# A decoder block in fp32 on one core: five running sums per pair of down-projection blocks, copies on ScalarE, the residual stored over three blocks

## Chip, cores and metric

One core of one Trainium2 chip runs the whole program in one launch. The metric is the device time of one execution in microseconds, the median of several runs. The core has TensorE (matrix products, "PE", with its weight loads "PEld"), VectorE ("DVE"), ScalarE ("ACT"), GpSimd ("POOL") and SyncE ("SP"), each with a queue that is worked off in order. Data moves between chip memory (HBM) and the on-chip SBUF by 16 DMA engines. Matrix products land in PSUM, eight banks of 128 x 512 fp32.

## The reference

A decoder block over 512 tokens of width 2048: RMS norm, one input projection, two kinds of attention, an output projection, then a gated feed-forward layer and a last RMS norm. Only the end matters here:

```python
h = h + mixed @ w_out[l]
hn2 = rmsnorm(h, norm2_g[l])
h = h + (jax.nn.silu(hn2 @ w_gate[l]) * (hn2 @ w_up[l])) @ w_down[l]
return rmsnorm(h, final_g)
```

`w_gate` and `w_up` are 2048 x 5632, `w_down` is 5632 x 2048, all fp32. Tokens stand in the free dimension, so an activation tile is 128 features x 512 tokens; token halves are called LO and HI (256 each).

## The kernel before

**Numbers.** Every fp32 operand is split into a high and a low part (`h` by a ScalarE copy that rounds, line 142 or 165; `l` by a VectorE subtraction, line 145 or 169). A product is three matmuls: high x high, low x high, high x low (`mm`, lines 1210 to 1212). A matmul is 128 x 128 weights by 256 or 512 columns.

**Gate and up blocks.** The 5632 hidden features are 44 blocks f = 0 to 43. The gate and up products of a block are computed by a scheme with seven products P1 to P7 instead of eight, with sums of weight quarters and of activation quarters. A block reads four raw weight units of 128 x 1024 (A11, A21, A22, A12). VectorE forms the sums of weight quarters in place (`comb`, line 811); `fetch` (line 815) is another way to do it: a GpSimd DMA that adds a piece from HBM onto a tile in SBUF. A product is two "halves" of 12 matmuls each. Products P2 and P3 go on in the banks of P1 and P6, and ScalarE seeds the banks of P6 and P7 with copies (line 1362). `after(f, name)` takes the banks out: for P2, VectorE multiplies bank P1 by the row of reciprocal norms `r2` into `g` (line 1282), one half later. The order of the seven products is `ORDER0` for f = 0, `ORDER1` (P2 third) for f = 1 and 2, `ORDER` (P2 sixth) afterwards.

**Splits ahead.** `next_half` splits the weights of three halves ahead before the matmuls of a half are issued, and starts loads of raw units on SP (`load_to`, five buffers). `later(n, f)` runs `f` n halves later, `soon(n, f)` n products of the down stage later. This is the only order there is: each engine's queue holds its instructions as these calls made them.

**Down stages.** Hidden features are collected over four blocks. For each group of four, the product with `w_down` follows: for the first group sixteen plain blocks in f = 4 (`down`), for nine later groups a stage at f = 8, 12, ..., 40 of eight pairs of output blocks k = 0 to 7, again with seven products each (`down7`), six matmuls per product, the products of neighbouring k interleaved. Four banks serve a k: after P1 ScalarE copies bank b1 into b2, after P6 b2 into b3 (the seeds). Results go to a staging tile of 128 x 1024 (`stg`, three buffers): ScalarE copies three of four quarters (line 1150), VectorE adds two times to make the others (line 1147), and a GpSimd DMA adds the tile onto `kept_sums[k]` in HBM (line 1166, 512 KB). `hidden_terms` makes the activation sums for a stage in a tile of the same three buffers.

**The residual.** `put_away(nb)` scales one of 16 residual blocks `hs` on VectorE and stores it in `kept_sums` by SP (lines 1316 to 1322). Eight are done one per half after product P5 of f = 1, eight after P5 of f = 2; the last one closes the pool of `hs` and opens the pool with the staging tiles. `bring_back(nb)` loads them again in f = 41 and 42, and `last` adds the products of the last group and normalises.

```python
        elif name == "P7":
            soon(1, add(s[3], b3, s[1]))
        elif name == "P3":
            soon(1, add(s[1], b2, s[1]))
        elif name == "P4":
            soon(1, copy(s[2], b3))
            soon(2, lambda: pool_e.dma_start(kept_sums[k], sums[k], accum_op=OP.add))
```

Of the kernel before, what the change touches and what calls it, by code (L numbers as in the profile page):

```python
# [11 lines left out]
F32 = mybir.dt.float32  # L12
# [4 lines left out]
S = 512  # L17
# [57 lines left out]
def block_kernel(ctx: ExitStack, tc: tile.TileContext, xt, wst, wdn, smalls, wg, w2c, bias, ident_in, out):  # L75
# [6 lines left out]
    wp = ctx.enter_context(tc.tile_pool(name="wp", bufs=1))  # L82
    ps = ctx.enter_context(tc.tile_pool(name="ps", bufs=1, space=bass.MemoryType.PSUM))
    mem = ctx.enter_context(tc.tile_pool(name="mem", bufs=1, space=bass.MemoryType.DRAM))
    kept_sums = [mem.tile([128, 2 * S], F32, name=f"sums{k}") for k in range(8)]

    def placed(pool, n, at, **kw):

# [714 lines left out]
    def quad_jobs(f, order):  # L803

        u = units.index(("quad", f, 0))

        def q(i, k):
            return raws[u + i][:, 512 * k:512 * k + 512]

        def comb(o, x):  # L810
            return lambda: dve.tensor_tensor(o(), o(), x(), op=OP.add)  # L811

        def fetch(o, i, k):

            return lambda: pool_e.dma_start(o(), wst[u + i][:, 512 * k:512 * k + 512], accum_op=OP.add)

        def nxt(i):
            return lambda: load_to(u + 4 + i + 1)

        r = {}  # L820
        for k in range(2):
            A11, A21, A22, A12 = (lambda i=i, k=k: q(i, k) for i in range(4))

            if f == 0:
                r["P1", k] = Job(A11, load=None if k else nxt(-1), post=fetch(A11, 1, k))
                r["P5", k] = Job(A21, post=fetch(A21, 0, k))
                r["P7", k] = Job(A11)
                r["P2", k] = Job(A12)
                r["P4", k] = Job(A22, prep=comb(A12, A21))
                r["P6", k] = Job(A21)  # L830
                r["P3", k] = Job(A12)
            else:
                r["P1", k] = Job(A11, post=comb(A11, A21))
                r["P4", k] = Job(A22, post=comb(A21, A22))
                r["P6", k] = Job(A22, prep=comb(A22, A11))
                r["P5", k] = Job(A21)
                r["P7", k] = Job(A11)
                r["P2", k] = Job(A12)
                r["P3", k] = Job(A12, prep=comb(A12, A22))
        if f + 1 < FB:  # L840
            if f == 0:
                r["P6", 1].post = nxt(2)
                r["P3", 1].post = nxt(3)
            else:
                r["P7", 1].post = nxt(RB - 3)
                r["P3", 1].post = nxt(RB - 1)
        else:
            r["P7", 1].post = lambda: load_fin(RB - 2)
            r["P3", 1].post = lambda: load_fin(RB)
        r["P1", 0].even = f == 2 or f % 2 == 1  # L850
        return [r[p, k] for p in order for k in range(2)]
# [4 lines left out]
    ORDER1 = ("P1", "P4", "P2", "P6", "P5", "P7", "P3")  # L856

    def order(f):
        return ORDER0 if not f else ORDER1 if f < 3 else ORDER

    def dn_job(p, nb):
        return Job(lambda: dn[p, nb], post=load_dn)
# [235 lines left out]
    banks["P5"] = ps.tile([128, 512], F32, tag="o", name="P5")  # L1098
    dbanks = {}
    SEEDED = ("P6", "P7")  # L1100

    def product(f, name):
        key = {"P2": "P1", "P3": "P6" if f else "P3"}.get(name, name)
# [25 lines left out]
    def down7(p, k, name, wh, wl):  # L1129

        if not roles:
            seed = ps.tile([128, 512], F32, tag="misc", name="pd")
            pe.matmul(seed[:, :256], ones, sm[:, :1].to_broadcast([128, 256]), start=True, stop=True)
            roles.append((banks["P3"], banks["P4"], seed, dbanks[1]))
            roles.append((banks["P1"], banks["P5"], banks["P7"], banks["P6"]))
        b1, b2, b3, b4 = (b[:, :256] for b in roles[k % 2])
        o = {"P1": b1, "P2": b1, "P6": b2, "P3": b2, "P7": b3, "P4": b3, "P5": b4}[name]
        th, tl = parts[name]
        for i in range(2):
            c = slice(128 * i, 128 * i + 128)  # L1140
            mm(o, wh[:, c], wl[:, c], th[:, i, :], tl[:, i, :], i == 0 and name in ("P1", "P5"), i == 1)
        if name == "P2":
            sums[k] = st["pool"].tile([128, 1024], F32, tag="stg", name="stg", bufs=3)
        s = [sums[k][:, 256 * q:256 * q + 256] if k in sums else None for q in range(4)]

        def add(o, a, b):
            return lambda: dve.tensor_tensor(o, a, b, op=OP.add)

        def copy(o, a):
            return lambda: act.activation(o, a, AF.Copy)  # L1150

        if name == "P1":
            copy(b2, b1)()
        elif name == "P6":
            copy(b3, b2)()
        elif name == "P2":
            soon(1, copy(s[0], b1))
        elif name == "P5":
            soon(1, copy(s[1], b4))
        elif name == "P7":  # L1160
            soon(1, add(s[3], b3, s[1]))
        elif name == "P3":
            soon(1, add(s[1], b2, s[1]))
        elif name == "P4":
            soon(1, copy(s[2], b3))
            soon(2, lambda: pool_e.dma_start(kept_sums[k], sums[k], accum_op=OP.add))  # L1166

    def hidden_terms(i, top, bot):

        x3 = st["x3"]  # L1170
        hl = [[a[:, 12:16, :].rearrange("p t (i c) -> p t i c", c=256)[:, :, i, :] for a in (ah, al)],
              [a.rearrange("p (t i c) -> p t i c", i=2, c=256)[:, :, i, :] for a in x3]]
        t = st["pool"].tile([128, 1024], F32, tag="stg", name="tt", bufs=3)
        t = [t[:, 256 * q:256 * q + 256] for q in range(4)] + [t]

        def two(q):
            return t[4][:, 512 * q:512 * q + 512].rearrange("p (t c) -> p t c", c=256)

        botv = bot.rearrange("p (t c) -> p t c", c=256)

        def hi(w, a, b, src):
            act.activation(hl[w][0][:, a:b, :], src, AF.Copy)

        def lo(w, a, b, src):
            dve.tensor_tensor(hl[w][1][:, a:b, :], src, hl[w][0][:, a:b, :].bitcast(F32), op=OP.subtract)

        def s1():
            dve.tensor_tensor(t[0], top[:, LO], top[:, HI], op=OP.subtract)
            dve.tensor_tensor(t[1], bot[:, HI], top[:, HI], op=OP.subtract)
            hi(0, 0, 2, botv)  # L1190
            hi(1, 2, 3, top[:, None, LO])

        def s2():
            dve.scalar_tensor_tensor(t[2], t[1], -1.0, top[:, LO], op0=OP.mult, op1=OP.subtract)
            dve.scalar_tensor_tensor(t[3], t[2], -1.0, bot[:, LO], op0=OP.mult, op1=OP.subtract)
            hi(0, 2, 4, two(0))
            lo(0, 0, 2, botv)
            lo(1, 2, 3, top[:, None, LO])

        def s3():  # L1200
            hi(1, 0, 2, two(1))
            lo(0, 2, 4, two(0))

        def s4():
            lo(1, 0, 2, two(1))

        return [s1, s2, s3, s4]
# [40 lines left out]
    def after(f, name):  # L1248
# [30 lines left out]
            sub(u[:, LO], x("P7"), u[:, LO])  # L1279
            add(u[:, HI], x("P7"), g[:, HI])  # L1280
        elif name == "P2":
            dve.tensor_tensor(g[:, LO], x("P1"), st["r2"][:, LO], op=OP.mult)  # L1282
            if f == FB - 1:
                finish(f, g, u, LO)
        elif name == "P3":
# [7 lines left out]
    def down(ph, nb):  # L1293
# [9 lines left out]
                   al[:, 12 + i, c], i == 0, i == PH - 1)  # L1303

        def add():
            t = st["pool"].tile([128, 1024], F32, tag="stg", name="stg", bufs=3)[:, :512]
            act.activation(t, p, AF.Copy, scale=1.0 if nb < 8 else -1.0)
            pool_e.dma_start(mem_at(nb), t, accum_op=OP.add)

        later(1, add)  # L1310

    def mem_at(nb):
        c = 512 * (nb // 8)
        return kept_sums[nb % 8][:, c:c + 512]

    def put_away(nb):
        h = hs[:, nb, :]
# [1 line left out]
            dve.tensor_tensor(h, h, st["inv"], op=OP.mult)  # L1319
        else:  # L1320
            dve.scalar_tensor_tensor(h, h, -1.0, st["inv"], op0=OP.mult, op1=OP.mult)
        sp.dma_start(mem_at(nb), h)
        if nb == KB - 1:
            rest["hsp"].close()
            st["dnp"] = ExitStack()
            pool = st["pool"] = st["dnp"].enter_context(tc.tile_pool(name="dnp", bufs=1))
            st["x3"] = [placed(pool, 3 * S, at, name="x3" + x) for x, at in (("h", MH), ("l", ML))]
            for name, x, n in (("P2", 0, 0), ("P3", 0, 1), ("P5", 0, 2), ("P7", 0, 3), ("P6", 1, 0), ("P4", 1, 1), ("P1", 1, 2)):
                parts[name] = tuple((b[:, S * n:S * n + S] if x else a[:, 12 + n, :]).rearrange("p (i c) -> p i c", c=256)
# [2 lines left out]
    def bring_back(nb):  # L1332
        if nb == 0:
            st["dnp"].close()
            st["hs"] = ctx.enter_context(tc.tile_pool(name="fin", bufs=1)).tile([128, KB, S], F32, name="hs")
        sp.dma_start(st["hs"][:, nb, :], mem_at(nb))

    for kind, a, b in sched:
        if kind == "d":
# [10 lines left out]
            continue  # L1350
        f, name = a, b
        product(f, name)
        if name == "P5" and f in (1, 2):
            for n in range(8):
                later(n, lambda nb=8 * (f - 1) + n: put_away(nb))
        if name == "P5" and f in (FB - 3, FB - 2):
            for n in range(8):
                later(n, lambda nb=8 * (f - FB + 3) + n: bring_back(nb))
        if f and name in ("P1", "P6"):
            o = {"P1": "P6", "P6": "P7"}[name]  # L1360
            st[o] = banks[o]
            act.activation(st[o][:, :256], st[name][:, :256], AF.Copy)
# [172 lines left out]
```

## Time and profile before

| | |
|---|---|
| time, median of 3 runs | 2181.99 us (2180.06 to 2184.23) |
| the profiled execution | 2184.53 us, span 2182.8 us |
| granted TensorE clock | 0.998 |
| PE / DVE / ACT / POOL busy | 99% / 78% / 54% / 5% |
| moved by DMA | 282.65 MB |

A share of busy time is over the span. Ends of matmuls are modelled, so they overlap in the rows (281 ns each, one every 113 ns). In a group of instructions stand: line, engine, operation, output and inputs by the program's names, shapes, count, then busy us, mean ns of one, the engine's idle time just before them and what ended it. In a row of waits stand: who waited, for whom, us in total, times, longest us. In a timeline row: start, duration, and in brackets the idle time before it and who ended it.

### The profile page before, as it was taken

Reading aid. Unit: us, or ns where it says so; the run is one execution under the profiler, and the core shown is the slowest. Engines: PE = TensorE matmul, PEld = TensorE weight load, DVE = VectorE, ACT = ScalarE, POOL = GpSimd, SP = SyncE. Lnnn points to the kernel's source line nnn. Section 1 sums busy time; section 2 is a strip of 40 time slices with the busy share of each in tenths; the row PEclk is TensorE's granted clock in tenths of the full one; section 3 lists DMA queues with packets and bytes.
Section 4 is the critical chain, followed back from the end, with each engine's and each line's share of the span. In section 5 each row is a group of like instructions: output and inputs, shape, how many; then the busy total and the mean of one; then the engine's idle time right before and its main releaser. Section 6 shows DMA issues by size and latency. Waiting matters only on the chain.

```text
span 2182.8 us, 40518 instructions
## 1 busy us (share of the span) xinstructions
PE 2152.6 (99%) x15346; PEld 2005.0 (92%) x15346; DVE 1701.4 (78%) x3624; ACT 1187.8 (54%) x2767; POOL 119.1 (5%) x139
## 2 busy tenths in 40 slices
PE   9999999999999999999999999999999999999997
PEld 8888888888888889999999999999999999999997
DVE  6755565456668588938989898999989898989886
ACT  6544444244444256445656656565756566565656
POOL 0000000000000000020000001010000000010103
PEclk9999999999999999999999999999999999999999
DMA  6442222322225333573563738374655647383762
GB/s 233 151 132 83 87 80 68 102 77 82 88 68 167 102 96 98 185 167 105 133 168 105 174 110 192 98 173 118 150 135 134 163 108 172 110 192 98 169 208 97
DMA packets 88787, 282.65 MB, mean 129 GB/s; under 512 B 9616, under 2 KB 12304, under 8 KB 88592
## 3 DMA queue, kind: packets, MB, share of 16 engines
q1 hardware_dynamic: 75056, 236.49, 35.3%
q0 software_dynamic: 13392, 43.52, 11.6%
q8 instruction: 120, 1.97, 0.4%
q14 instruction: 75, 0.61, 0.1%
q10 hardware_dynamic: 144, 0.07, 0.0%
HBM read 229.70 MB, written 50.33 MB: 128 GB/s over the span
## 4 chain that ended last, share of the span: by engine, by line
PE 79%; DVE 10%; DMA 5%; ACT 3%; issue 3%; ACTq 0%; DVEq 0%
PE P L1210 12%; PE P L1211 12%; PE P L1212 12%; PE pp L196 7%; PE pp L198 7%; PE pp L197 7%; DMA sums<-stg 5%; DVE wl L145 3%; PE pab L196 3%; PE pab L197 3%; PE pab L198 3%; DVE wl L169 1%; PE pt L567 1%; DVE raw L811 1%; ACT wh L165 1%
## 5 line engine op out<-in xcount | busy, mean ns | idle before, releaser
L142 ACT ACTIVATE wh<-raw 128x512 fp32r<-128x512 f32 x888 | 536.8, 626 | 352.8 <-DVE raw L811 169.6
L145 DVE TENSOR_TENSOR wl<-raw,wh 128x512 fp32r<-128x512 f32 x888 | 596.5, 686 | 77.2 <-ACT wh L142 75.2
L1210 PE MATMUL P<-ah,wh 128*128 128x256 f32 x1552 | 436.4, 281 | 9.1 <-ACT P L1150 7.0
L1212 PE MATMUL P<-ah,wl 128*128 128x256 f32 x1552 | 431.4, 278 | 0.7 <-DVE wl L145 0.7
L1211 PE MATMUL P<-al,wh 128*128 128x256 f32 x1552 | 431.1, 278 | 0.0
L1210 PEld LDWEIGHTS P<-ah,wh 128*128 128x128 f32 x1552 | 291.1, 188 | 15.8 <-ACT P L1150 13.6
L1212 PEld LDWEIGHTS P<-ah,wl 128*128 128x128 f32 x1552 | 291.3, 188 | 0.9 <-DVE wl L145 0.9
L1211 PEld LDWEIGHTS P<-al,wh 128*128 128x128 f32 x1552 | 291.3, 188 | 0.0
L196 PE MATMUL pp<-ah,wh 128*128 128x512 f32 x640 | 260.6, 407 | 0.0
L198 PE MATMUL pp<-ah,wl 128*128 128x512 f32 x640 | 251.0, 392 | 0.0
L197 PE MATMUL pp<-al,wh 128*128 128x512 f32 x640 | 250.1, 391 | 0.0
L811 DVE TENSOR_TENSOR raw<-raw 128x512 f32<-128x512 f32 x346 | 238.4, 689 | 6.5
L165 ACT ACTIVATE wh<-raw 128x256 fp32r<-128x256 f32 x432 | 159.8, 410 | 26.2 <-DVE raw L888 25.3
L169 DVE TENSOR_TENSOR wl<-raw,wh 128x256 fp32r<-128x256 f32 x432 | 166.9, 419 | 9.2 <-ACT wh L165 8.5
L198 PEld LDWEIGHTS pp<-ah,wl 128*128 128x128 f32 x640 | 120.2, 188 | 28.3 <-DVE wl L145 0.4
L196 PEld LDWEIGHTS pp<-ah,wh 128*128 128x128 f32 x640 | 120.5, 188 | 19.9 <-DVE tmp L368 0.5
L197 PEld LDWEIGHTS pp<-al,wh 128*128 128x128 f32 x640 | 120.6, 189 | 19.5
L554 ACT ACTIVATE e<-e,st 128x512 f32<-128x512 f32 (+1 forms) x96 | 53.7, 560 | 124.2 <-DVE st L548 124.2
L1166 POOL DMA_DIRECT2D sums<-stg x72 | 62.4, 867 | 1022.5 <-ACT stg L1150 826.6
L1210 PE MATMUL P<-B11h,wh 128*128 128x256 f32 x352 | 98.9, 281 | 3.2 <-DVE ft L1282 2.3
L1210 PE MATMUL P<-x3h,wh 128*128 128x256 f32 x360 | 100.7, 280 | 0.0
L1212 PE MATMUL P<-x3h,wl 128*128 128x256 f32 x360 | 100.4, 279 | 0.0
(331 smaller groups left out, 5317.9 us busy)
## 6 DMA issues: line engine op xcount, KB each, us to landing
raw<-in_wst_dram SPq DMA_DIRECT2D x382, 512.0 KB, 3.8
sums<-stg POOLq DMA_DIRECT2D x72, 512.0 KB, 7.9
bias<-in_bias_dram SPq DMA_DIRECT2D x16, 320.0 KB, 3.0
xc<-in_xt_dram SPq DMA_DIRECT2D x16, 256.0 KB, 3.7
rawd<-in_wdn_dram SPq DMA_DIRECT2D x16, 256.0 KB, 3.8
hs<-in_xt_dram SPq DMA_DIRECT2D x16, 256.0 KB, 6.0
sums<-hs SPq DMA_DIRECT2D x16, 256.0 KB, 3.8
sums<-stg POOLq DMA_DIRECT2D x16, 256.0 KB, 5.1
```

Of the source, the lines that this page charges most:

```text
L142: act.activation(self.h, self.src(), AF.Copy)
L145: dve.tensor_tensor(self.l, self.src(), self.h.bitcast(F32), op=OP.subtract)
L165: act.activation(h, src(), AF.Copy)
L169: dve.tensor_tensor(l, src(), h.bitcast(F32), op=OP.subtract)
L196: pe.matmul(o, wh, mh, start=start, stop=False)
L197: pe.matmul(o, wh, ml, start=False, stop=False)
L198: pe.matmul(o, wl, mh, start=False, stop=stop)
L811: return lambda: dve.tensor_tensor(o(), o(), x(), op=OP.add)
L1166: soon(2, lambda: pool_e.dma_start(kept_sums[k], sums[k], accum_op=OP.add))
L1210: pe.matmul(o, wh, mh, start=start, stop=False, skip_group_check=True)
L1211: pe.matmul(o, wh, ml, start=False, stop=False, skip_group_check=True)
L1212: pe.matmul(o, wl, mh, start=False, stop=stop, skip_group_check=True)
```

## The change

- **Sums.** `kept_sums[k]` has five blocks of 128 x 256 instead of four quarters. The two sums that VectorE made in the staging tile are no longer made: what P7 and P3 leave in their banks is copied by ScalarE, and block 2, which both output blocks of the pair contain, is added when the residual comes back. Staging is in three tiles: `a` (P2 and P5, blocks 1 and 2, three buffers), `b` (P7 and P3, blocks 3 and 4, two buffers), `c` (P4, block 0, two buffers), each with a DMA of its own: 256, 256 and 128 KB. `hidden_terms` takes two `a` tiles.
- **Residual.** `put_away` runs in f = 1 (four), f = 2 (six) and f = 3 (six), one per two halves. Behind the last, block 2 of each `kept_sums` is set to zero: a GpSimd memset and eight SP stores. A residual block lies in two separate 1 KB rows. `bring_back` loads it and adds block 2 to its HI half with a GpSimd DMA.
- **Weights of f = 1 to 3.** They have `ORDER1`, and the sum A11 + A21 for P7 is made by `fetch` instead of VectorE (P6 takes its sum from A11 and A21 directly).
- **Bank P1.** For f > 0, ScalarE copies it to `g` right behind product P2; VectorE then multiplies `g` in place.

```diff
-    kept_sums = [mem.tile([128, 2 * S], F32, name=f"sums{k}") for k in range(8)]
+    kept_sums = [mem.tile([128, 5, 256], F32, name=f"sums{k}") for k in range(8)]
...
+            elif f < 4:
+                r["P1", k] = Job(A11)
+                r["P4", k] = Job(A22, post=comb(A21, A22))
+                r["P6", k] = Job(A22, prep=lambda a=A11, b=A21, o=A22: dve.tensor_tensor(o(), a(), b(), op=OP.add),
+                                 post=fetch(A11, 1, k))
+                r["P5", k] = Job(A21)
+                r["P7", k] = Job(A11)
+                r["P2", k] = Job(A12)
+                r["P3", k] = Job(A12, prep=comb(A12, A22))
...
-        return ORDER0 if not f else ORDER1 if f < 3 else ORDER
+        return ORDER0 if not f else ORDER1 if f < 4 else ORDER
...
+    AWAY = {(1, "P5"): (0, 4, 0), (2, "P1"): (4, 6, 4), (3, "P1"): (10, 6, 1)}
...
-        if name == "P2":
-            sums[k] = st["pool"].tile([128, 1024], F32, tag="stg", name="stg", bufs=3)
+        def stage(x, n, bufs):
+            sums[x] = st["pool"].tile([128, n, 256], F32, tag="stg" + x, name="stg", bufs=bufs)
+
+        def add(x, q, n):
+            return lambda s=sums[x]: pool_e.dma_start(kept_sums[k][:, q:q + n, :], s, accum_op=OP.add)
...
         elif name == "P2":
-            soon(1, copy(s[0], b1))
+            stage("a", 2, 3)
+            soon(1, copy(sums["a"][:, 0, :], b1))
         elif name == "P5":
-            soon(1, copy(s[1], b4))
+            soon(1, copy(sums["a"][:, 1, :], b4))
+            soon(2, add("a", 1, 2))
         elif name == "P7":
-            soon(1, add(s[3], b3, s[1]))
+            stage("b", 2, 2)
+            soon(1, copy(sums["b"][:, 0, :], b3))
         elif name == "P3":
-            soon(1, add(s[1], b2, s[1]))
+            soon(1, copy(sums["b"][:, 1, :], b2))
+            soon(2, add("b", 3, 2))
         elif name == "P4":
-            soon(1, copy(s[2], b3))
-            soon(2, lambda: pool_e.dma_start(kept_sums[k], sums[k], accum_op=OP.add))
+            stage("c", 1, 2)
+            soon(1, copy(sums["c"][:, 0, :], b3))
+            soon(2, add("c", 0, 1))
...
-            dve.tensor_tensor(g[:, LO], x("P1"), st["r2"][:, LO], op=OP.mult)
+            dve.tensor_tensor(g[:, LO], g[:, LO], st["r2"][:, LO], op=OP.mult)
...
+            zero = pool.tile([128, 256], F32, tag="s2", name="zero", bufs=2)
+            pool_e.memset(zero, 0.0)
+            for k in range(8):
+                sp.dma_start(kept_sums[k][:, 2, :], zero)
...
-        sp.dma_start(st["hs"][:, nb, :], mem_at(nb))
+        h = st["hs"][:, nb, :].rearrange("p (t c) -> p t c", c=256)
+        sp.dma_start(h, mem_at(nb))
+        pool_e.dma_start(h[:, 1, :], kept_sums[nb % 8][:, 2, :], accum_op=OP.add)
...
+        if f and name == "P2":
+            act.activation(st["g"][:, LO], st["P1"][:, :256], AF.Copy)
```

More of the change, by code (lines that the diff above doesn't have):

```diff
@@ L1141, in down7 @@
             mm(o, wh[:, c], wl[:, c], th[:, i, :], tl[:, i, :], i == 0 and name in ("P1", "P5"), i == 1)
-        if name == "P2":
-            sums[k] = st["pool"].tile([128, 1024], F32, tag="stg", name="stg", bufs=3)
-        s = [sums[k][:, 256 * q:256 * q + 256] if k in sums else None for q in range(4)]
-        def add(o, a, b):
-            return lambda: dve.tensor_tensor(o, a, b, op=OP.add)
         def copy(o, a):
             return lambda: act.activation(o, a, AF.Copy)
+        def stage(x, n, bufs):
+            sums[x] = st["pool"].tile([128, n, 256], F32, tag="stg" + x, name="stg", bufs=bufs)
+        def add(x, q, n):
+            return lambda s=sums[x]: pool_e.dma_start(kept_sums[k][:, q:q + n, :], s, accum_op=OP.add)
         if name == "P1":
@@ L1172, in hidden_terms @@
               [a.rearrange("p (t i c) -> p t i c", i=2, c=256)[:, :, i, :] for a in x3]]
-        t = st["pool"].tile([128, 1024], F32, tag="stg", name="tt", bufs=3)
-        t = [t[:, 256 * q:256 * q + 256] for q in range(4)] + [t]
+        tt = [st["pool"].tile([128, 2, 256], F32, tag="stga", name="tt", bufs=3) for _ in range(2)]
+        t = [tt[q // 2][:, q % 2, :] for q in range(4)]
         def two(q):
-            return t[4][:, 512 * q:512 * q + 512].rearrange("p (t c) -> p t c", c=256)
+            return tt[q]
         botv = bot.rearrange("p (t c) -> p t c", c=256)
@@ L1305, in add @@
         def add():
-            t = st["pool"].tile([128, 1024], F32, tag="stg", name="stg", bufs=3)[:, :512]
-            act.activation(t, p, AF.Copy, scale=1.0 if nb < 8 else -1.0)
+            t = st["pool"].tile([128, 2, 256], F32, tag="stga", name="stg", bufs=3)
+            act.activation(t, p.rearrange("p (t c) -> p t c", c=256), AF.Copy, scale=1.0 if nb < 8 else -1.0)
             pool_e.dma_start(mem_at(nb), t, accum_op=OP.add)
@@ L1312, in mem_at @@
     def mem_at(nb):
-        c = 512 * (nb // 8)
-        return kept_sums[nb % 8][:, c:c + 512]
+        return kept_sums[nb][:, 1:5:3, :] if nb < 8 else kept_sums[nb - 8][:, 0:4:3, :]
     def put_away(nb):
@@ L1321, in put_away @@
             dve.scalar_tensor_tensor(h, h, -1.0, st["inv"], op0=OP.mult, op1=OP.mult)
-        sp.dma_start(mem_at(nb), h)
+        sp.dma_start(mem_at(nb), h.rearrange("p (t c) -> p t c", c=256))
         if nb == KB - 1:
@@ L1352, in block_kernel @@
         product(f, name)
-        if name == "P5" and f in (1, 2):
-            for n in range(8):
-                later(n, lambda nb=8 * (f - 1) + n: put_away(nb))
+        if (f, name) in AWAY:
+            first, n, at = AWAY[f, name]
+            for i in range(n):
+                later(at + 2 * i, lambda nb=first + i: put_away(nb))
         if name == "P5" and f in (FB - 3, FB - 2):
```

## The prediction

> **What bounds the kernel now.** I read the page first, then the waits of TensorE's weight loads, then nine windows of one stage, then the timelines inside it.
>
> ```profile
> span 2182.8 us, 40518 instructions
> PE 2152.6 (99%) x15346; PEld 2005.0 (92%) x15346; DVE 1701.4 (78%) x3624; ACT 1187.8 (54%) x2767; POOL 119.1 (5%) x139
> q1 hardware_dynamic: 75056, 236.49, 35.3%
> ```
>
> TensorE is the bound, and the change neither adds nor takes a matmul. So it can only move the time in which TensorE waits or runs below its best pitch. The weight loads show that time best, because their ends are not modelled:
>
> ```profile
> PEld P L1210 <- ACT P L1150: 13.6, 28, 1.0
> PEld pd L1210 <- ACT pd L1150: 5.7, 7, 1.4
> PEld P L1210 <- issue: 4.1, 9, 0.5
> PEld P L1210 <- ACT P L1362: 2.2, 2, 1.4
> PEld P L1212 <- DVE wl L145: 0.9, 1, 0.9
> ACT stg L1150 <- DMA sums<-stg: 41.0, 29, 3.0
> ```
>
> The first two rows, 19.3 us in 35 waits, are the down-projection's seeds: ScalarE copies one bank into the next before TensorE goes on in it. The third is the start of a gate/up block. The fourth and fifth are the crowded blocks f = 1 and 2. Together 26.5 us, about 1.2% of the span. The last row says why ScalarE is late at least at times: it stands before a staging tile that an old transfer still reads. Now the pace, in a window of a down stage, one of plain blocks, and the sum over nine windows that hold the nine stages:
>
> ```profile
> 1183.00:1222.00 39.00, 38.13 (x316) 37.43 (x315) 35.30 (x93) 28.44 (x90) 5.20 (x6) 1.00 0.75 171
> 1350.00:1389.00 39.00, 39.00 (x345) 39.00 (x345) 33.95 (x59) 20.83 (x41) 0.86 (x1) 1.00 0.48 136
> sum 351.00, PE 339.50 PEld 332.01 DVE 315.64 ACT 252.12 POOL 45.02; mean PE 37.72 PEld 36.89 DVE 35.07 ACT 28.01 POOL 5.00
> ```
>
> Columns are PE, PEld, DVE, ACT, POOL, clock, DMA share, GB/s. A plain matmul takes 39/345 = 0.113 us; the stage does 29 fewer in the same time, 3.3 us lost. The clock is 1.00 in both. In a stage VectorE is 90% busy (315.64 of 351), ScalarE 72%.
>
> **The change part by part.**
>
> *The block's start (A).*
>
> ```profile
> 1164.21 0.28 PE L1210 MATMUL P<-ah,wh 128*128 128x256 f32 x1
> 1165.03 0.35 PE L1210 MATMUL P<-B11h,wh 128*128 128x256 f32 x1 [0.32 <-DVE ft L1282]
> 1165.46 0.28 PE L1210 MATMUL P<-B11h,wh 128*128 128x256 f32 x1
> 1171.82 0.28 PE L1210 MATMUL P<-ah,wh 128*128 128x256 f32 x1
> L1362 ACT ACTIVATE P<-P 128x256 f32<-128x256 f32 x86 | 31.6, 368 | 84.0 <-PE P L1212 84.0
> ```
>
> Bank P1 is held until VectorE's late multiply (L1282) has read it; an L1210 comes every third matmul, so 1165.03 should have been 1164.55. After the change ScalarE reads the bank right behind product P2. One copy is 0.37 us by the L1362 row, and product P3 (24 matmuls, 2.7 us) runs meanwhile. ScalarE already stops twice per block at such copies; what queues behind the third are weight splits for three halves (4.1 us) ahead. VectorE's multiply stays, now out of SBUF, with nobody on TensorE behind it. I take the whole 4.1 us. In the last block the copy lies ahead of the final product: at most 0.4 us back.
>
> *The sums (B).* Per pair of blocks k VectorE loses two adds, ScalarE gains two copies.
>
> ```profile
> L1147 DVE TENSOR_TENSOR stg<-P,stg 128x256 f32<-128x256 f32 x108 | 45.6, 422 | 14.1 <-ACT wh L165 6.1 <-PE P L1212 3.6 <-DVE stg L1147 0.5
> L1150 ACT ACTIVATE stg<-P 128x256 f32<-128x256 f32 x144 | 54.1, 375 | 48.1 <-DMA sums<-stg 41.0 <-PE P L1212 5.4 <-PE pd L1212 1.4
> ...
> 1189.73 0.28 PE L1212 MATMUL P<-ah,wl 128*128 128x256 f32 x1
> 1190.13 0.38 PE L1210 MATMUL P<-ah,wh 128*128 128x256 f32 x1
> 1195.06 0.28 PE L1212 MATMUL P<-ah,wl 128*128 128x256 f32 x1
> 1195.76 0.39 PE L1210 MATMUL P<-ah,wh 128*128 128x256 f32 x1 [0.42 <-ACT P L1150]
> 1195.98 0.28 PE L1211 MATMUL P<-al,wh 128*128 128x256 f32 x1
> ...
> 1193.55 0.42 ACT L165 ACTIVATE wh<-s 128x256 fp32r<-128x256 f32 x1 [1.07 <-DVE s L885]
> 1218.66 0.38 ACT L1150 ACTIVATE stg<-P 128x256 f32<-128x256 f32 x1 [2.06 <-DMA sums<-stg]
> ```
>
> The 144 adds at 0.42 us are 61 us: VectorE falls from 90% to about 73%. The 144 copies at 0.375 us are 54 us: ScalarE rises from 72% to 87% at most. It now copies after each of the seven products of a k, and each copy waits for TensorE; between two products (6 matmuls, 0.68 us) it needs one copy and, on average, one 256-wide split. A seed has two products of slack, 1.4 us. So ScalarE keeps up, with little to spare.
>
> Three kinds of wait make up the 19.3 us. The first of a stage (1190.13, 0.29 us too late) comes before any add and stays: 9 x 0.29 = 2.6. The second (1195.76, 0.59 late) follows a ScalarE that waited 1.07 us for VectorE, which two adds had held up: 9 x 0.59 = 5.3, of which I take 4.8. The other 11.4 us go with staging tiles as at 1218.66. Each removed wait also saves a slow restart (1195.76 to 1195.98 is 0.22, not 0.11).
>
> Will the tiles come free? A k is 42 matmuls, 4.75 us.
>
> ```profile
> sums<-stg POOLq DMA_DIRECT2D x72, 512.0 KB, 7.9
> sums<-stg POOLq DMA_DIRECT2D x16, 256.0 KB, 5.1
> L1166 POOL DMA_DIRECT2D sums<-stg x72: 862/862/891, 1075.8 to 2070.5; - x72
> L1308 POOL DMA_DIRECT2D sums<-stg x16: 862/862/881, 935.3 to 985.6; - x16
> ```
>
> Now a tile is filled from product P2 to P4, nine products (6.2 us), then 0.5 us to the issue and 7.9 to land: 14.6 us against three tiles' 14.3. That is the wait. After: tile a 2.0 + 0.5 + 5.1 = 7.6 against 14.3; b 0.7 + 0.5 + 5.1 = 6.3 against two tiles' 9.5; c under 5.6 against 9.5. By latency b has 3 us to spare. GpSimd issues three instead of one, 3 x 0.86 of 4.75 us: it fits.
>
> The Trainium skill speaks against this (DMA: Bandwidth & Descriptors, "Anatomy of one DMA — SWDGE (gpsimd) path"): each such transfer has about 2.0 us fixed beside its bytes at 436 GB/s, so estimates from that page are 3.2 us for the one and 7.5 us for the three, more than a k. The L1308 row disagrees if that is read as time in a row: 16 transfers left 3.4 us apart and landed 5.1 us after issue, so they overlapped.
>
> The Trainium skill also warns (SBUF — State Buffer, "SBUF: two separate sides") that VectorE can lock GpSimd out while it writes descriptors. The 891 ns maximum at a VectorE 90% busy shows nothing of it.
>
> The engines' time is another matter:
>
> ```profile
> q0 software_dynamic: 258, 0.95, 97.1%
> q0 software_dynamic: 2304, 4.20, 44.7%
> q1 hardware_dynamic: 1152, 4.20, 38.2%
> ```
>
> These are 1225 to 1230 us (512 KB transfers, queue full), 932 to 992 (the sixteen 256 KB ones) and 1182 to 1222 (weights in a stage). An accumulated MB costs 5 x 0.971/0.95 = 5.1 us of all sixteen engines at best and 60 x 0.447/4.20 = 6.4 in smaller pieces; a weight MB 3.6 there, 3.26 over the run (35.3% of 2182.8 for 236.49). Per k the change moves 0.66 MB for 0.52: 3.35 + 1.7 = 5.0 us at the low end; at the high end 4.2 + 1.9 = 6.1, and more if the 1 KB rows of tile c cost as much a piece as 2 KB rows. Against 4.75. So the engines run full, and a backlog grows by 0.3 to 1.4 us per k over eight k. I take 5.2, near the full-queue row, because a backlog hides the gaps between transfers; then up to 3.6 us pile up against b's 3 us, and half of the 11.4 us go: 5.7. With 17.5 restarts at 0.11 (1.9), B = 4.8 + 5.7 + 1.9 = 12.4.
>
> *The blocks f = 1 to 3 (C).* Sixteen stores with a VectorE multiply each ran one per half (12 matmuls, 1.36 us); now one per two halves, over three blocks. Six adds of raw tiles leave VectorE for six GpSimd transfers issued from products P6 on. Their data is wanted four halves (5.4 us) later.
>
> ```profile
> L811 DVE TENSOR_TENSOR raw<-raw 128x512 f32<-128x512 f32 x346 | 238.4, 689 | 6.5
> raw<-in_wst_dram POOLq DMA_DIRECT2D x4, 256.0 KB, 4.3
> ```
>
> The like of them landed in 4.3 us, and ScalarE's lead of 4.1 us covers a late one; uncovered it costs some 1 us each. Six adds are 4.1 us less on VectorE. Of the 3.1 us of waits I take 2.4, and pay 0.5 for transfers. The zeros (one memset, eight SP stores behind the last residual store) hold SP for an estimated 6 to 8 us at the end of f = 3, before the next 256 KB loads; first use of the new pool is some 11 us off. Strided rows in f = 4 and on return I set at 0.4.
>
> *Pitch (D).* 1165.46 to 1171.82 is 18 groups at 0.353 us instead of 0.340: after a wait TensorE stays 4% slow. Up to the next stage (17 us) that is 0.6 x 9 = 5.8; inside a stage 3.3 - (19.3 + 35 x 0.11)/9 = 0.7, x 9 = 6. Whether it goes with the wait is open: 0 to 12, I take 4.
>
> Sum: 4.1 + 12.4 + 2.4 + 4 - 1.3 = 21.6. The profiled execution took 2184.53 us, so 2163; that one lies 2.5 above the median 2181.99 of the three runs (2180.06 to 2184.23), so I say **2160**.
>
> **The rivals.**
> *Slower: the DMA engines set the pace of the down stage.* At 6.1 us per k, eight k take 48.8 us for about 40 now; some 4 us are taken up by tiles in flight at both ends, so 5 us x 9 = 43, less A and C: 2182 + 43 - 6.5 = 2218. It breaks even near 5.6 us per k. For it: the priced rows. Against it: the full-queue row. The fixed cost per transfer of the Trainium skill's page (DMA: Bandwidth & Descriptors), paid in a row, would end here too. Chance 0.16.
> *ScalarE becomes the bound of the stage*: its copies delay the seeds as VectorE did, B and D vanish, A and C stay: about 2176. For it: 87%; against: 1.4 us of slack. Chance 0.18.
> *The change doesn't do what it says*: waits only move to the next engine, within 4 us of 2182. Chance 0.06.
> *The forecast*, waits largely gone: 0.60, its own range 2144 to 2171: 37.5 us if all of A, C and D goes and B but for its first waits (4.1 + 19.6 + 3.1 + 12 - 1.3), 11.4 with half of B and no D.
>
> **How the numbers follow.** 0.2%, 4.4 us, is about what can be told from no change. Faster 0.60 + 0.18 = 0.78, same 0.06, slower 0.16. The range runs from 2144 over the ScalarE case up to a mild DMA case, 2188 (5.65 us per k).
>
> **What would show it.** Right: the weight loads' "issue" row of nine is gone; ScalarE's 41.0 us before staging tiles fall under 15; L1150's 35 waits fall to 10 to 20; DVE in the nine windows near 270 us, ACT near 300. Wrong: landings of the 256 KB accumulates above 8 us with ScalarE waiting for them, DMA share near 1.0 in the stage; or a ScalarE without idle time ahead of late seeds.

## The result: 0.33% faster, a third of the forecast

| | before | after |
|---|---|---|
| median, us | 2181.86 (2179.57 to 2184.23, 8 runs) | 2174.97 (2169.29 to 2179.9, 8 runs) |
| ratio, 95% interval | | 0.9967 [0.9954, 0.998] |
| profiled execution, us | 2184.53, span 2182.8 | 2175.91, span 2174.1 |

6.9 us were gained where 21.9 were forecast. The prediction's range (2144 to 2188) and its sign hold; its number is 15 us too low.

The lines of the page after that answer to those shown of before:

```profile
span 2174.1 us, 41104 instructions
...
PE 2145.2 (99%) x15346; PEld 2001.7 (92%) x15346; DVE 1653.8 (76%) x3474; ACT 1235.5 (57%) x2954; POOL 268.9 (12%) x306
```

VectorE is 48 us less busy and ScalarE 48 us more: the work of the adds has moved. The waits of the weight loads and of ScalarE's staging copies, after (engine, line, what was waited for: us in total, times, longest):

```profile
PEld P L1224 <- ACT P L1384: 10.1, 11, 1.1
PEld P L1224 <- ACT P L1153: 8.0, 10, 0.9
...
PEld P L1224 <- ACT stg L1321: 1.6, 1, 1.6
...
ACT stg L1153 <- DMA sums<-stg: 0.3, 1, 0.3
```

Set beside the waits of before, three things went as forecast: the "issue" row of nine is gone, ScalarE's 41.0 us before staging tiles are 0.3, and the 35 waits for seeds of the down-projection (then L1150, now L1153) are 10. One thing did not: the first row. Product P6's seed in a gate/up block (then L1362, 2.2 us in 2 waits, now L1384) costs 10.1 us in 11. That is nine new waits of 0.8 to 1.0 us in place of nine of 0.5.

The nine windows of the down stages, first and sum (columns as before: PE, PEld, DVE, ACT, POOL, clock, DMA share, GB/s), and DMA queues and landings in 1185 to 1222 us, one stage:

```profile
1061.00:1100.00 39.00, 38.45 (x325) 38.17 (x324) 33.31 (x86) 33.63 (x106) 16.56 (x19) 1.00 0.91 204
...
sum 351.00, PE 345.04 PEld 341.64 DVE 304.23 ACT 300.33 POOL 145.63; mean PE 38.34 PEld 37.96 DVE 33.80 ACT 33.37 POOL 16.18
```

```profile
q0 software_dynamic: 2663, 4.09, 66.9%
q1 hardware_dynamic: 1046, 3.77, 30.2%
...
sums<-stg POOLq DMA_DIRECT2D x15, 256.0 KB, 7.4
...
sums<-stg POOLq DMA_DIRECT2D x7, 128.0 KB, 6.9
```

TensorE is busier by 5.5 us over the nine windows, ScalarE stands at 300 as forecast. The engines of the DMA are 97% full through the stage (66.9 and 30.2), the sign that the prediction named for its slower rival, and still ScalarE waits for a tile only once, 0.3 us.

### The profile page after: what moved, and what is told of

The parts are those of the page before. It is cut to its first block, busy times and chain, and to the rows that moved or that the text cites. A ratio compares the mean times of both kernels' runs of the same rounds, so it can differ in the third digit from the quotient of the medians.

```text
span 2174.1 us, 41104 instructions
## 1 busy us (share of the span) xinstructions
PE 2145.2 (99%) x15346; PEld 2001.7 (92%) x15346; DVE 1653.8 (76%) x3474; ACT 1235.5 (57%) x2954; POOL 268.9 (12%) x306
## 4 chain that ended last, share of the span: by engine, by line
PE 82%; DVE 10%; issue 3%; ACT 3%; DMA 1%; SPq 0%; DVEq 0%; ACTq 0%; POOL 0%; POOLq 0%
PE P L1224 13%; PE P L1226 12%; PE P L1225 12%; PE pp L196 7%; PE pp L198 7%; PE pp L197 7%; DVE wl L145 4%; PE pab L198 3%; PE pab L196 3%; PE pab L197 3%; DVE raw L811 2%; ACT wh L142 2%; PE pd L1224 1%; PE pd L1226 1%; PE pd L1225 1%
## 5 line engine op out<-in xcount | busy, mean ns | idle before, releaser
L142 ACT ACTIVATE wh<-raw 128x512 fp32r<-128x512 f32 x888 | 527.4, 624 | 351.4 <-DVE raw L811 196.9
L145 DVE TENSOR_TENSOR wl<-raw,wh 128x512 fp32r<-128x512 f32 x888 | 596.1, 685 | 103.0 <-ACT wh L142 100.7
L1159 POOL DMA_DIRECT2D sums<-stg x216 | 187.7, 920 | 886.7 <-ACT P L1153 721.7
L811 DVE TENSOR_TENSOR raw<-raw 128x512 f32<-128x512 f32 x334 | 229.8, 688 | 6.2
L1153 ACT ACTIVATE stg<-P 128x256 f32<-128x256 f32 x252 | 95.0, 381 | 15.1 <-PE P L1226 3.6
L196 PE MATMUL pab<-ah,wh 128*128 128x512 f32 x256 | 100.3, 392 | 0.0
```

Source lines behind the costliest of these rows:

```text
L142: act.activation(self.h, self.src(), AF.Copy)
L145: dve.tensor_tensor(self.l, self.src(), self.h.bitcast(F32), op=OP.subtract)
L196: pe.matmul(o, wh, mh, start=start, stop=False)
L1159: return lambda s=sums[x]: pool_e.dma_start(kept_sums[k][:, q:q + n, :], s, accum_op=OP.add)
```

## Where the missing 15 us are: the experiments

Differences are against the runs of the kernel before in the same group of runs. The medians of before were 2181.71, 2184.68, 2185.63 and 2186.38 us in the four groups, so a difference between two groups is sure to some 4 us only.

| run | what it is | median, us | ratio to before [95%] | against before, us |
|---|---|---|---|---|
| after | the change | 2174.97 | 0.9967 [0.9954, 0.998] | -6.9 |
| e1 | after, no copy of bank P1 | 2162.76 | 0.9908 [0.9895, 0.9922] | -19.0 |
| e2 | after, Silu behind P6's seed | 2158.23 | 0.9897 [0.988, 0.9915] | -23.5 |
| e3 | before, with the sums alone | 2165.69 | 0.992 [0.9907, 0.9934] | -16.0 |
| e5 | after, f = 1 to 3 as before | 2176.22 | 0.997 [0.9957, 0.9982] | -5.5 |
| e4 | before, with the copy alone | 2194.70 | 1.0055 [1.0042, 1.0068] | +10.0 |
| e6 | e1, Silu behind P6's seed | 2157.21 | 0.9876 [0.9864, 0.9889] | -27.5 |
| e7 | e1, zeros later | 2161.55 | 0.9896 [0.9884, 0.9909] | -23.1 |
| e8 | before, two small tiles | 2171.08 | 0.9945 [0.9932, 0.9958] | -13.6 |
| e9 | e6, zeros later | 2153.65 | 0.9849 [0.9835, 0.9863] | -32.0 |
| e10 | before, Silu behind P6's seed | 2178.73 | 0.9968 [0.9957, 0.9979] | -6.9 |
| e11 | e1 again | 2163.09 | 0.9892 [0.9876, 0.9908] | -22.5 |
| e12 | e9 with the copy | 2165.12 | 0.9909 [0.9894, 0.9924] | -21.3 |

e1, e2, e3 and e5 are one group, e4 and e6 to e8 one, e9 to e11 one, e12 one. The profiled executions of e2, e4 and e9 (2167.23, 2203.25 and 2158.41 us) lie 5 to 9 us above the medians of their kernels, so their profiles are read for the kind of their waits; a sum taken from them is said to be one. Those of the others lie within 3 us.

**Theory and rivals.** The theory after the result: the copy of bank P1 moved a wait instead of removing it, since what is late in that block is VectorE, and the copy only lets TensorE run further ahead to the next result that hangs on VectorE. Rivals: the sums gain less than forecast (DMA contention or ScalarE's load), or the early blocks lose.

**e1: the copy taken out.**

```diff
-            dve.tensor_tensor(g[:, LO], g[:, LO], st["r2"][:, LO], op=OP.mult)
+            dve.tensor_tensor(g[:, LO], x("P1"), st["r2"][:, LO], op=OP.mult)
...
-        if f and name == "P2":
-            act.activation(st["g"][:, LO], st["P1"][:, :256], AF.Copy)
```

> The changed kernel without ScalarE's copy of bank P1: VectorE multiplies straight out of the bank again. Theory (a late VectorE sets the time there, and the copy only moves TensorE's stop from the start of a block to the seed of P6, where it stands behind the Silu): the nine waits for L1282's like come back at 0.4 to 0.5 us, the nine waits of 0.84 to 0.93 us for the seed (L1384) go, so about 4 us faster than the changed kernel, 2171 us. Rival (the seed is late because of the sums or the residual, and the copy does save its 4 us): the seed's waits stay and 4 us come on top, 2179 us.

12.2 us faster than after (between two groups), three times what the theory said; against before the gain is then 19.0 us, of the forecast's size. Its waits:

```profile
PEld P L1224 <- ACT P L1153: 5.9, 13, 0.9
PEld P L1224 <- issue: 4.4, 9, 0.5
...
PEld P L1224 <- ACT stg L1321: 1.4, 1, 1.4
PEld P L1224 <- ACT P L1382: 1.3, 2, 1.0
```

The nine old waits are back, 4.4 us, and the nine new ones are gone. The timelines of the same block show the trade. After (start, us, engine, line; in brackets the idle time and its releaser):

```profile
1162.18 0.28 PE L1224 MATMUL P<-B11h,wh 128*128 128x256 f32 x1
1163.22 0.42 DVE L1296 TENSOR_TENSOR ft<-ft,r 128x256 f32<-128x256 f32 x1
1167.13 0.42 DVE L1304 TENSOR_TENSOR ft<-ft,r 128x256 f32<-128x256 f32 x1
1167.59 0.63 ACT L1232 ACTIVATE ft<-ft 128x512 f32<-128x512 f32 x1 [1.28 <-DVE ft L1304]
1168.13 0.37 ACT L1384 ACTIVATE P<-P 128x256 f32<-128x256 f32 x1
1168.55 0.38 PE L1224 MATMUL P<-ah,wh 128*128 128x256 f32 x1 [0.76 <-ACT P L1384]
```

And e1:

```profile
1160.58 0.42 DVE L1296 TENSOR_TENSOR ft<-P,r 128x256 f32<-128x256 f32 x1
1161.15 0.35 PE L1224 MATMUL P<-B11h,wh 128*128 128x256 f32 x1 [0.32 <-DVE ft L1296]
1164.50 0.42 DVE L1304 TENSOR_TENSOR ft<-ft,r 128x256 f32<-128x256 f32 x1
1164.96 0.63 ACT L1232 ACTIVATE ft<-ft 128x512 f32<-128x512 f32 x1 [1.28 <-DVE ft L1304]
1165.50 0.37 ACT L1382 ACTIVATE P<-P 128x256 f32<-128x256 f32 x1
```

L1296 is VectorE's late multiply out of bank P1. From it to L1304, the multiply that the Silu needs, VectorE takes 3.91 us in one kernel and 3.92 in the other, working without a pause. So P6's seed, which stands behind the Silu on ScalarE, starts 4.9 us after L1296 in both. In e1 TensorE cannot begin the block before L1296 has read the bank: it begins 0.57 us after its start, loses 0.32 there, and finds the seed ready. With the copy it begins 1.04 us ahead of L1296, and stands 0.76 us for the seed.

By these rows an earlier TensorE alone would not have met that wait. In e1 the seed ends at 1165.87 us and its product's weights are loaded at 1166.76, so 0.89 us are to spare; and the copy brings TensorE there only 0.72 us sooner (its matmuls in after start 1.51 us later than e1's ahead of the block, 0.79 just ahead of the seed). The rest is that the copy itself makes VectorE late, a block earlier. After:

```profile
1140.54 0.38 ACT L1380 ACTIVATE ft<-P 128x256 f32<-128x256 f32 x1 [1.88 <-PE P L1226]
1140.82 1.66 ACT L142 ACTIVATE wh<-raw 128x512 fp32r<-128x512 f32 x3
1141.48 0.69 DVE L145 TENSOR_TENSOR wl<-raw,wh 128x512 fp32r<-128x512 f32 x1 [1.03 <-ACT wh L142]
```

And e1:

```profile
1137.61 0.63 ACT L142 ACTIVATE wh<-raw 128x512 fp32r<-128x512 f32 x1 [0.47 <-PE P L1225]
1138.84 0.68 DVE L145 TENSOR_TENSOR wl<-raw,wh 128x512 fp32r<-128x512 f32 x1
```

The copy (L1380) stands 1.88 us for the end of product P2, with three weight splits behind it on ScalarE; e1 has the first of them done by then. VectorE needs that split for the low part (L145) and stands 1.03 us for it. Up to there its instructions start 1.5 us later than e1's, as TensorE's do; from there to the block above, 2.64. So VectorE has lost 1.13 us on TensorE, and 0.72 + 1.13 - 0.89 = 0.96 us is what the weight load waits for the seed. The pages of the three pairs agree: VectorE's idle time before L145 for ScalarE is 100.7 us in after and 90.6 in e1, 84.3 in e4 and 75.2 in before, 95.0 in e12 and 89.6 in e9 (e4 and e9 in their long executions). This is read from the traces; no run takes the splits alone from behind the copy.

**e4: the copy alone, on the kernel before.** The same two edits the other way round.

> The kernel before with ScalarE's copy of bank P1 alone, and the multiply out of SBUF. Prediction's step A: the nine waits of 0.5 us go and nothing takes their place, 2181.9 - 4.1 = 2177.8. Theory now: the bank is free early, but product P6's seed, which ScalarE copies behind the Silu, comes late in turn (0.8 to 0.9 us, nine times, the later one because the Silu waits for VectorE), and in the down stages the first seed gets later too: 2 to 12 us slower than before, 2184 to 2194. Rival: the copy hurts only where ScalarE carries the five sums' copies as well; then before with the copy is within 2 us of before.

10.0 us slower than before, so the copy hurts without the sums too; step A's 2177.8 and the rival both fall.

```profile
PEld P L1210 <- ACT P L1150: 16.0, 25, 0.9
PEld pd L1210 <- ACT pd L1150: 11.5, 13, 2.7
PEld P L1210 <- ACT P L1364: 11.3, 11, 1.7
```

The third row is the same as in after: eleven waits for P6's seed (L1364 here), where before had two. The row of nine for the block's start is gone here too.

**e2 and e6: the seed taken from behind the Silu,** with the copy (e2) and without (e6).

```diff
-        act.activation(g, g, AF.Silu)
-        last4 = f >= FB - PH
+        def silu():
+            act.activation(g, g, AF.Silu)
+
+        if f < FB - 1:
+            later(0, silu)
+        else:
+            silu()
```

> The changed kernel with the Silu of a block issued one half later, so that it stands behind the seed in ScalarE's queue instead of ahead of it. Theory (the two waits that are left in every four blocks, 0.84 to 0.93 us at P6's seed and 0.83 us early in the down stage, are a seed that stands behind a Silu that waits for VectorE): both go, 18 waits with their restarts, some 17 us, 2158 us, and more if the slow pitch behind them goes too. Rival (VectorE's throughput itself is the limit there): TensorE catches up with VectorE a little later, waits for split weights appear instead, and no more than 5 us are gained, 2170 us.

> The changed kernel without the copy of bank P1 and with the Silu issued behind P6's seed. If the late seed was the Silu's doing and the copy is no help by itself, this has neither wait of the two: the nine waits of 0.5 us at the block's start are left (4 us), and the time is that of the kernel without the copy (2162.8) less 0 to 3 us: 2160 to 2163. If the Silu's place matters for itself (the stage's first seed was 0.3 to 0.5 us late nine times), 2157 to 2160. Rival: the later Silu makes VectorE's products of g late and the split weights with them: 2164 to 2168.

e2's median is what the theory said. Its profile shows the rival's wait beside it, though:

```profile
PEld P L1226 <- DVE wl L145: 11.3, 17, 0.9
PEld P L1224 <- ACT P L1153: 4.1, 9, 0.5
```

The seed is no longer waited for; TensorE now stops in the same product for a low part of the weights, which VectorE makes (L145). e6 is the faster expected case, with fewer waits than any kernel before it:

```profile
PEld P L1226 <- DVE wl L145: 2.8, 5, 0.9
PEld P L1224 <- issue: 1.9, 6, 0.3
...
PEld P L1224 <- ACT P L1153: 0.9, 3, 0.3
```

The Silu's place helps twice: it also stood ahead of the first seed of each down stage, whose row falls from 5.9 to 0.9.

**e12 and e9: is the copy worth anything once the seed is early?** Both have the Silu behind the seed and the zeros later (e7); e12 has the copy.

> The changed kernel whole, the copy of bank P1 included, with the Silu behind P6's seed and the zeros stored in the fifth block: beside the like without the copy (ratio 0.9849) it tells what the copy is worth once the seed no longer stands behind the Silu. By the prediction's step A, the nine waits at the block's start that are left (2.3 us) go: 0.9835 to 0.984. By the theory that VectorE is late in that block anyway, they come back as waits for VectorE's split weights, as in the run with the Silu alone moved: 0.985 to 0.987.

> The changed kernel without the copy of bank P1, with the Silu behind P6's seed and with the zeros stored one per half in the fifth block: all three mends together. If each acts by itself, its ratio to before is that of the first two (0.9876) less 0.0005 to 0.001: about 0.987, 28 us under before. Rival: the Silu's place had already made room for the late weights, and the zeros bring nothing more: 0.9876 within 0.0005.

e12 is slower than e9, by 0.9909 to 0.9849, and slower than both theories had it (0.985 to 0.987 was the worse one). Its waits are those the second theory named:

```profile
PEld P L1226 <- DVE wl L145: 10.4, 14, 0.9
PEld P L1224 <- ACT P L1153: 3.1, 8, 0.5
```

VectorE's rows in e12's block, and where TensorE stops:

```profile
1160.38 0.42 DVE L1301 TENSOR_TENSOR ft<-ft,r 128x256 f32<-128x256 f32 x1
1165.24 0.69 DVE L145 TENSOR_TENSOR wl<-raw,wh 128x512 fp32r<-128x512 f32 x1
1165.98 0.39 PE L1226 MATMUL P<-ah,wl 128*128 128x256 f32 x1 [0.67 <-DVE wl L145]
```

This split comes 4.9 us after the multiply (L1301 here), and TensorE comes for it 0.67 us too soon. The copy holds up the splits here too: it stands 1.88 us for product P2 at 1137.84. So the wait was met in three places on one queue: at the bank (0.3 us), at the seed (0.8), at the split (0.7). The first is the cheapest, and the only one ahead of which no copy has held VectorE up. How much the copy costs with the Silu moved is not settled: 11 us between e12 and e9, but 1 between the medians of e2 and e6 (4 when each is taken against its before), each from different groups. In no pair did it gain.

e9 is the fastest kernel of the study, 32 us under before and 1.2% faster than after in its ratio. It did better than expected by 4 us.

**e10: the Silu's place alone, on the kernel before.**

> The kernel before, where only the Silu is issued behind P6's seed. The theory that P6's seed is late because it stands behind a Silu that waits for VectorE: in the kernel before that is a matter of two seeds (2.2 us) and of ScalarE's lateness at the start of a down stage (9 times 0.3 us), so 2 to 6 us faster than before, with the nine waits at the block's start no longer than they were. Rival: with two adds per pair of blocks VectorE is the engine that is late, the Silu's place makes its next products later still, and the time is that of before within 2 us, or slower.

Faster by 6.9 us, a little more than the theory's range, but not by its reason alone.

```profile
PEld P L1210 <- ACT P L1150: 12.4, 15, 1.3
PEld pd L1210 <- ACT pd L1150: 10.6, 9, 2.9
PEld P L1210 <- issue: 2.9, 9, 0.3
PEld P L1212 <- DVE wl L145: 2.4, 4, 0.9
```

The two P6 seeds are out of the list and the nine waits are shorter, but the four rows sum to 28.3 us, against 26.5 before. What the profiled execution gained (4.6 us) is in the pace, below; the run does not say why.

**e3 and e8: the sums.** e3 is before with the five sums, their tiles and the zeros, and nothing else. e8 keeps four sums and VectorE's adds, and only halves the tiles:

```diff
-            sums[k] = st["pool"].tile([128, 1024], F32, tag="stg", name="stg", bufs=3)
-        s = [sums[k][:, 256 * q:256 * q + 256] if k in sums else None for q in range(4)]
+            sums[k] = [st["pool"].tile([128, 512], F32, tag="stg" + x, name="stg", bufs=3) for x in "ab"]
+        s = [sums[k][q // 2][:, 256 * (q % 2):256 * (q % 2) + 256] if k in sums else None for q in range(4)]
...
             soon(1, add(s[1], b2, s[1]))
+            soon(2, put(0))
...
-            soon(2, lambda: pool_e.dma_start(kept_sums[k], sums[k], accum_op=OP.add))
+            soon(2, put(1))
```

> The kernel before with the five sums and the smaller staging tiles alone (with the zeros that they need behind the last residual store): no copy of bank P1, the residual and the weights of f = 1 to 3 as before. Theory (the sums are what gains, as the prediction's part B said, 12 us): 2170 us, ScalarE's 41 us before staging tiles gone, the nine waits at a block's start as before. Rival (the parts need each other): within 4 us of before.

> The kernel before with its four sums in two staging tiles of two blocks each (three of each, the same bytes in SBUF), each with a transfer of its own as soon as its half is filled; VectorE still makes its two adds per k, memory holds four sums, the bytes moved are the same. Theory of step B (half and more of the gain is the tiles' lifetime): ScalarE's 41 us before staging tiles fall under 5, TensorE's waits for seeds from 19.3 us to 6 to 9, and the time is 2181.9 less 8 to 14 = 2168 to 2174. Rival: the gain of the five sums (16 us) is VectorE's relief; then the staging waits go but the time falls by less than 5 us: 2177 to 2182.

The sums bring 16.0 us alone, more than the 12 expected. e8 brings 13.6, at the upper end of the lifetime theory, so most of step B is that a tile is given back sooner; what e3 has beyond that, the two adds that VectorE loses above all, is some 2 us by the medians and 5 by the ratios, about what two groups can differ. The first row is e8's, the second (another kernel) e3's:

```profile
PEld P L1214 <- ACT P L1153: 10.9, 19, 0.9
```

```profile
PEld P L1215 <- ACT P L1144: 5.2, 10, 0.9
```

In the two stages of e8 that were read there are two such waits each (at 1188.64 and 1194.26 us; at 1307.14 and 1312.76); in the stage of e3 that was read, one (1187.34). So the prediction's three kinds of wait come apart: e8 removes the third, e3 the second too, and the first stays. e6 removes that one.

**e5 and e7: the early blocks.** e5 takes back f = 1 to 3 and keeps the rest. e7 is e1 with the eight zero stores one per half in f = 5:

```diff
...
+        if (f, name) == (5, "P1"):
+            zero = st["pool"].tile([128, 256], F32, tag="s2", name="zero", bufs=2)
+            pool_e.memset(zero, 0.0)
+            for k in range(8):
+                later(k, lambda k=k: sp.dma_start(kept_sums[k][:, 2, :], zero))
```

> The changed kernel with the blocks f = 1 to 3 as before: the residual stored one block per half in f = 1 and 2, sums of raw weights by VectorE, the order of products of f = 3 as before. Theory (stores over three blocks gained nothing: the stops of 0.74, 0.82 and 1.35 us went and others of 0.53, 0.71, 0.44, 1.05 and 1.57 us came, the last one because the zeros on SP hold up weights of f = 4): 1 to 3 us faster than the changed kernel, 2173 us. Rival (the spreading does gain its 2.4 us): 2177 us.

> The changed kernel without the copy of bank P1, and the eight stores of zeros issued one per half in the fifth block instead of eight in a row behind the last residual store. If they held SP and so made the first down weights late (one stop of 1.4 to 1.6 us, and a slower pitch for some blocks behind it): 2159 to 2161.5 against 2162.8, and no stop of TensorE for a staging copy near 934 us. Rival: the load comes late for another reason (the pool's first use); the stop stays and the time is 2162.8 within 1 us.

The early blocks' change is worth 1.3 us with the copy (after against e5, two groups) and 2.9 without (e1 against e3, one group), so the theory that it cost 1 to 3 us falls. One stop in after is their doing:

```profile
925.25 3.76 SPq L1343 DMA_DIRECT2D sums<-zero  x8
929.10 5.25 SPq L793 DMA_DIRECT2D rawd<-in_wdn_dram  x4
931.82 0.63 ACT L142 ACTIVATE wh<-rawd 128x512 fp32r<-128x512 f32 x1 [3.89 <-DMA rawd<-in_wdn_dram]
935.12 0.39 PE L1224 MATMUL P<-ah,wh 128*128 128x256 f32 x1 [1.41 <-ACT stg L1321]
```

SP stores the zeros for 3.8 us, the next down weights start behind them, ScalarE stands 3.9 us for their high part, and TensorE 1.4. At the weight loads that stop is 1.6 us in after, 1.4 in e1 and 0.4 in e7; e7's time is 1.2 us under e1's across groups, just short of what was expected and within what two groups can differ. The rest of the stop, and so the whole cause, is not shown.

**e11: e1 once more,** to read e9 and e10 beside it.

> The changed kernel without the copy of bank P1 once more, beside the two above on one chip, so that the Silu's place and the zeros are read against it and not across chips. Its ratio to before was 0.9908; 0.990 to 0.9915 here. The kernel with the Silu moved and the zeros later should then be 5 to 9 us faster than this one; the rival (the differences seen before were between chips) gives less than 3.

e11's own ratio, 0.9892, is a little under the 0.990 to 0.9915 expected. e9 is 9.4 us faster than e11 in one group, a little more than the 5 to 9 expected: the Silu's place and the zeros together are a real gain. What the zeros' place brings alone is not shown.

## Why the prediction was right or wrong

**A, the block's start: wrong in sign, and as large as the whole miss.** The step that failed is "VectorE's multiply stays, now out of SBUF, with nobody on TensorE behind it. I take the whole 4.1 us." The multiply itself is free, but VectorE's queue goes on from it without a pause to L1304 and to the splits of the same product, and TensorE is behind those. The sentence ahead of it failed too: "what queues behind the third are weight splits for three halves (4.1 us) ahead" counts their lead up to TensorE, but VectorE takes them first. It stood 1.03 us for one and was 1.1 us later from there on. Instead of +4.1 the copy is worth -10.0 (e4, one group) to -12.2 (e1 and after, two groups). The forecast without A, 21.6 - 4.1 = 17.5 us, met 19.0 in e1 and 22.5 in e11. That it came so near is in part luck: B brought more than its 12.4, and D's 4 have no ground.

The waits explain most of that price, not all. Between the profiled executions of after and e1 the spans differ by 14.3 us: 9.3 stand in gaps of TensorE (27.5 against 18.2, in the table under D) and 4.7 in its slower pitch. The gaps are the seeds' 0.76 us for the bank's 0.32, the first seeds of the stages (L1153, 8.0 against 5.9 us), and the slow restarts behind them. The 4.7 have no wait of their own, and what sets them is open.

**B, the sums: right in place and size.** 16.0 us (e3) for 12.4; D is apart, below. Half of the 11.4 us of staging waits was to be left by a DMA backlog; none was. The engines did run full: 6.05 us per accumulated MB (0.669 x 37 / 4.09) and 2.96 per weight MB (30.2%, 3.77 MB), so 0.66 x 6.05 + 0.52 x 2.96 = 5.5 us per k, just under the 5.6 at which the slower rival was to break even. It did not bite because landings stayed at a median of 7.4 us, 8.7 at most: by the median tile b takes 0.7 + 0.5 + 7.4 = 8.6 of 9.5 us, so 0.9 us are left. Why they grew no further is not shown.

**VectorE in the nine windows** was to fall to 270 us and is at 304. The adds, 48.4 us of the 315.64 by their line L1147, left, but other work of its queue came into the same 39 us: the shown window has 86 instructions for the 94 of the same stage of before, not 16 fewer.

**C and E, the early blocks:** 2.4 less 0.9 in costs was forecast, 1.3 to 2.9 measured. One argument in it failed: "first use of the new pool is some 11 us off" covered the pool, but the zeros also held SP ahead of the down weights.

**D, the pitch: the 4 us have no ground.** From the starts of successive 256-column matmuls after 857 us one can sum what they lose over 113 ns: up to 125 ns apart as pitch, beyond that as gaps.

| profiled execution | gaps, us | slow pitch, us |
|---|---|---|
| before | 34.7 | 30.5 |
| after | 27.5 | 28.5 |
| e1 | 18.2 | 23.8 |
| e6 | 10.8 | 26.9 |
| e9 | 9.2 | 29.1 |
| e10 | 36.3 | 25.1 |

The gaps went with the changes; the slow pitch did not go with the gaps. e6, with a third of before's gaps, still loses 26.9 us to it, and e9, in an execution 4.8 us above its median, 29.1.

**The rivals.** DMA engines as the pace: not met, for the 0.9 us above. ScalarE as the bound: no; e6 has the same five copies and its stage seeds wait 0.9 us in all. The forecast's sign came true, while A's failure made the time (2175) look like the ScalarE rival's 2176 for another reason.

## What to carry to other kernels

Before a copy frees a buffer early, list what else the engine that frees it late has in its queue, and who waits for that: here that engine worked without a pause, the wait only moved down its queue, and the earliest place was the cheapest. List also what stands behind the copy on the engine that makes it: here weight splits, which the late engine needed next. An instruction that waits for another engine should not stand ahead of a seed that waits for nothing: moving the Silu, which costs no work, gained 7 us by itself and, with the zeros moved, 9 on top of the sums. Give back a staging tile as soon as its part is full; that alone was 13.6 us, with the same bytes and the same additions.

## What the hardware did that was not expected

DMA engines at 97% of a stage and landings of 7.4 us cost one wait of 0.3 us: here a full share was no wait, since the tile with the least room was back after 8.6 of 9.5 us. Matmuls of one shape run for long stretches at 117 to 118 ns and for others at 113 to 114, at a granted clock of 1.00 in both; 24 to 31 us hang on it in the profiled executions above. In e9 a slow stretch begins right behind a stop (some 780 matmuls from 934.12 us) or with a down stage (some 360 from 1061.37), and both of these end with no stop. What sets it was not found.
